# Softmax over 16384 rows of 512: the first load as even and odd partitions and the second as one DMA, both on SyncE's queue

## The chip, the cores and the metric

One core of one Trainium2 chip. The metric is the device time of one execution in microseconds (us). The kernel before takes 160.05 us (median; 159.97 to 160.12 in four runs). All runs were with a granted clock (the share of the full TensorE clock that the chip allowed) of 1.0. The profiled span, from the first to the last instruction, is about 1.4 us shorter than the time.

## The reference

```python
x: float32 [16, 1024, 512]
x_scaled = x / 2.0
exp_x = exp(x_scaled - max(x_scaled, axis=-1))
out = exp_x / sum(exp_x, axis=-1)            # float32
```

33.5 MB are read and 33.5 MB written, with a maximum, an exponential with its sum, and a multiplication in between.

## The kernel before

The 16384 rows are 128 rows in each of 128 partitions. They come in ten tiles of 3, 7, 13 and then 15 rows per partition, all in place in one arena of 98 rows in SBUF. VectorE takes the maximum, ScalarE the exponential with its sum, VectorE the reciprocal and the product, and SyncE (SP) issues the store. ScalarE (ACT) issues the loads, except load 0, which SyncE issues. Eight loads are issued at the start; the ninth and tenth reuse the arena's place and wait for stores. In the text "load 0" is the load of tile 0, and so on; a load has landed when its semaphore says that all of it is there. The first two are issued ahead of the program's entry barrier, the point at the start where the engines wait for one another. The code is cut:

```python
PLAN = [([3], 0), ([4, 3], 3), ([5, 4, 4], 10), ([5] * 3, 23), ...]   # chunks of rows, place in the arena
LAG = 2
SPREAD = 1

def issue_loads(begin, end):
    for t in range(begin, end):
        if t in behind:
            continue
        if t == 0:
            nc.sync.dma_start(out=sb(t), in_=dram(xf, t)).then_inc(ld[t], 16)
        elif t == SPREAD:
            r = tiles[t][1] - 1
            for p, q, lo, hi in ((0, P, 0, r), (0, 126, r, r + 1), (126, P, r, r + 1)):
                nc.scalar.dma_start(
                    out=sb(t)[p:q, lo:hi], in_=dram(xf, t)[p:q, lo:hi]
                ).then_inc(ld[t], 16)
        else:
            nc.scalar.dma_start(out=sb(t), in_=dram(xf, t)).then_inc(ld[t], 16)
...
for k in range(len(chunks) + LAG):          # VectorE
    if k < len(chunks):
        do_max(k)                           # waits for ld[t]
    if k >= LAG:
        do_mul(k - LAG)                     # waits for s_exp
for t in range(len(tiles)):                 # SyncE
    nc.sync.wait_ge(s_mul, last_chunk[t] + 1)
    nc.sync.dma_start(out=dram(of, t), in_=sb(t)).then_inc(...)
...
issue_loads(0, 2)                           # placed ahead of the entry barrier
...
issue_loads(2, len(tiles))                  # after it
```

So a row of load 0 (one partition's share) has 6144 bytes, of load 1 14336 (cut here into 12288 and 2048), of load 2 26624, of all others 30720.

## Time and profile before

| | before |
|---|---|
| time, us | 160.05 |
| bytes moved | 67.1 MB, 155.4 us at the 432 GB/s of the middle |
| VectorE, ScalarE busy | 83%, 60% of the span |
| load 0 issued, first row, landed | 0.00, 1.00, 6.2 us |
| load 1 issued, last row ended | 0.12, 8.28 us |
| last load's landing, last store issued | 127.6, 147.0 us |

The kernel is bound by its transfers; the prediction shows the lines. Two sources are used here. The views of the profile are quoted. The packet records of the trace (start, duration, size and queue of each row moved, without the engine's number) give times by row. Three sums over them, each divided by the 16 DMA engines, serve as a ledger:

- *idle*: time in which fewer than 16 rows were under way, from zero on;
- *slow*: what rows took beyond the usual for their size (84 ns for 2048 B, 158 for 4096, 234 for 6144, 460 for 12288, 535 for 14336, 987 for 26624, 1138 for 30720);
- the rest is rows at their usual pace, equal for all kernels but for 0.07 us.

Before: idle 1.18 us, all of it before 2 us, slow 0.57 up to 7 us, 0.45 from 7 to 10, 0.39 later.

### The profile page before, as it was taken

The page shows a single profiled execution, that of the slowest core. Times are in us where ns is not written, and L with a number is a line of the kernel's source. Part 1 is how long each engine was busy: PE and PEld are TensorE (multiplying, and loading weights), DVE is VectorE, ACT ScalarE, POOL GpSimd, SP SyncE. Part 2 cuts the span into 40 slices and gives each one's busy share as a digit, 9 for nine tenths or more (in the row PEclk, how much of TensorE's full clock was granted, in tenths as well). Part 3 has the DMA queues.
Part 4 walks back from the last instruction along what each step waited for, and adds up shares of the span by engine and source line. Part 5 has one row for each costly group of instructions (what it writes and reads, how often), then busy time and mean ns, then how long its engine had stood idle before and what let it go on. Part 6 is the DMA issues. An engine that isn't in the chain of part 4 may idle for free.

```text
span 158.6 us, 621 instructions
## 1 busy us (share of the span) xinstructions
DVE 131.4 (83%) x155; ACT 94.4 (60%) x257; POOL 0.2 (0%) x4
## 2 busy tenths in 40 slices
DVE  0466799999999999999999999996999389999000
ACT  0369197736874594669738797666566809763000
POOL 0000000000000000000000000000000000000000
DMA  7999999999999999999999999999999999999996
GB/s 268 449 373 430 414 431 466 435 407 399 466 443 389 434 463 448 418 444 426 442 426 434 426 426 442 426 441 411 457 395 472 395 473 395 472 395 465 395 472 263
DMA packets 3026, 67.13 MB, mean 423 GB/s; under 512 B 336, under 2 KB 336, under 8 KB 720
## 3 DMA queue, kind: packets, MB, share of 16 engines
q1 hardware_dynamic: 1584, 34.34, 50.6%
q10 hardware_dynamic: 1440, 32.77, 48.5%
q14 instruction: 2, 0.02, 0.0%
HBM read 33.55 MB, written 33.55 MB: 423 GB/s over the span
## 4 chain that ended last, share of the span: by engine, by line
DMA 52%; DVE 38%; issue 0%
DMA arena<-in_x_dram 38%; DVE stats L118 18%; DMA out_dram<-arena 14%; DVE arena L131 13%; DVE arena L138 7%; DVE recip L127 1%
## 5 line engine op out<-in xcount | busy, mean ns | idle before, releaser
L118 DVE TENSOR_REDUCE stats<-arena 128x5 f32<-128x2560 f32 (+2 forms) x27 | 72.2, 2676 | 14.6 <-DMA arena<-in_x_dram 14.6
L176 ACT ACTIVATE arena<-arena,stats 128x512 f32<-128x512 f32 x68 | 48.2, 710 | 23.4 <-DVE stats L118 23.4
L211 ACT ACTIVATE arena<-arena,stats x60 | 42.5, 710 | 20.7 <-ACTq L203 20.7
L138 DVE TENSOR_SCALAR arena<-arena,recip 128x512 f32<-128x512 f32 x93 | 38.6, 482 | 0.7
L131 DVE TENSOR_TENSOR arena<-arena,recip 128x2560 f32<-128x2560 f32 (+2 forms) x8 | 19.9, 2491 | 0.3
L176 ACT ACTIVATION_READ_ACCUMULATOR arena<-arena,stats 128x1 f32 x68 | 12.7, 187 | 0.0
L211 ACT ACTIVATION_READ_ACCUMULATOR arena<-arena,stats x60 | 11.2, 187 | 0.0
L127 DVE RECIPROCAL recip<-stats 128x5 f32<-128x5 f32 (+2 forms) x27 | 4.8, 177 | 0.0
L171 ACT ACT_TABLE_LOAD x1 | 1.3, 1283 | 5.7 <-issue 5.7
L252 POOL MEMSET const-bfloat16-1.0<- 128x1 bf16 x1 | 0.1, 101 | 0.0
L252 POOL MEMSET const-uint8-127<- 128x1 uint8 x1 | 0.1, 101 | 0.0
L252 POOL MEMSET const-float32-0.0<- 128x1 f32 x1 | 0.1, 98 | 0.2 <-issue 0.2
L252 POOL MEMSET const-float32-1.0<- 128x1 f32 x1 | 0.1, 98 | 0.0
## 6 DMA issues: line engine op xcount, KB each, us to landing
arena<-in_x_dram ACTq DMA_DIRECT2D x7, 3840.0 KB, 46.6
out_dram<-arena SPq DMA_DIRECT2D x7, 3840.0 KB, 22.7
arena<-in_x_dram ACTq DMA_DIRECT2D x1, 3328.0 KB, 14.3
out_dram<-arena SPq DMA_DIRECT2D x1, 3328.0 KB, 21.1
out_dram<-arena SPq DMA_DIRECT2D x1, 1792.0 KB, 18.2
arena<-in_x_dram ACTq DMA_DIRECT2D x1, 1536.0 KB
arena<-in_x_dram SPq DMA_DIRECT2D x1, 768.0 KB, 6.2
out_dram<-arena SPq DMA_DIRECT2D x1, 768.0 KB, 15.8
```

The costliest lines, as they stand in the source:

```text
L118: nc.vector.reduce_max(out=stats[:, b : b + c], in_=arena[:, a : a + c], axis=mybir.AxisListType.X, negate=True,)._wait_ge(ld[t], 48 if t ...
L127: nc.vector.reciprocal(out=recip[:, b : b + c], in_=stats[:, b : b + c])._wait_ge(s_exp, k + 1).then_inc(s_rec, 1)
L131: nc.vector.tensor_mul(out=arena[:, a : a + c], in0=arena[:, a : a + c], in1=recip[:, b : b + c].unsqueeze(2).to_broadcast([P, c, D]),)._w ...
L138: ins = nc.vector.tensor_scalar_mul(out=arena[:, a + r], in0=arena[:, a + r], scalar1=recip[:, b + r : b + r + 1],)
L171: nc.scalar.preload_act_table(mybir.ActivationFunctionType.Exp)
L176: ins = nc.scalar.activation(out=arena[:, a + r], in_=arena[:, a + r], func=mybir.ActivationFunctionType.Exp, bias=stats[:, b + r : b + r ...
L211: ins = nc.scalar.activation(out=data, in_=data, func=mybir.ActivationFunctionType.Exp, bias=stat, scale=0.5, accum_out=stat,)
L252: nc = _bacc.Bacc("TRN2", target_bir_lowering=False, num_devices=1)
```

## The change

Load 0 becomes two DMAs over the even and the odd partitions, load 1 a single one; all three go to SyncE's queue in order. The intent, as I read it, is to have the engines start evenly, so that the split over 126 and 2 partitions, which gave two late engines less work (they started load 0 at 1.62 and 1.75 us, the others at 1.00 to 1.25), isn't needed.

```diff
-SPREAD = 1
+HALVES = 2
             if t == 0:
+                for p in range(HALVES):
+                    nc.sync.dma_start(
+                        out=sb(t)[p:P:HALVES], in_=dram(xf, t)[p:P:HALVES]
+                    ).then_inc(ld[t], 16)
+            elif t == 1:
                 nc.sync.dma_start(out=sb(t), in_=dram(xf, t)).then_inc(ld[t], 16)
-            elif t == SPREAD:
-                r = tiles[t][1] - 1
-                for p, q, lo, hi in ((0, P, 0, r), (0, 126, r, r + 1), (126, P, r, r + 1)):
-                    nc.scalar.dma_start(
-                        out=sb(t)[p:q, lo:hi], in_=dram(xf, t)[p:q, lo:hi]
-                    ).then_inc(ld[t], 16)
...
-        )._wait_ge(ld[t], 48 if t == SPREAD else 16).then_inc(s_max, 1)
+        )._wait_ge(ld[t], 16 * HALVES if t == 0 else 16).then_inc(s_max, 1)
```

## The prediction

Passages that no trace or run of this case shows are cut from the text below, and the cuts are marked. -0.24 - 0.43 = -0.67 us gives 159.35, +0.18 - 0.43 = -0.25 us gives 159.77, and my forecast was 159.5. The -0.43 us itself stands on the trace (load 2's first rows took 1.34 to 1.49 us on all 16 engines, later ones 0.99, and nothing was lost at the step from 26624 to 30720 B). One correction from the same records: 14 engines have 84 ns rows just ahead of load 2, but two go straight from a 12288 B row to it, at 7.69 and 7.79 us (not 7.70), and lose the time too (1.49 and 1.45 us). The "two to four rows" of part 5 and the "20%" of the third rival are my estimates: the first from the 3.68 us between the issue of the first store (14.65) and its first row (18.33), the second assumed.

> **What bounds the kernel now.** I read the page first. It shows VectorE (DVE) busy for 83% of the span, ScalarE (ACT) for 60%, and the DMA row full in nearly every slice.
>
> ```profile
> span 158.6 us, 621 instructions
> DVE 131.4 (83%) x155; ACT 94.4 (60%) x257; POOL 0.2 (0%) x4
> DMA  7999999999999999999999999999999999999996
> DMA packets 3026, 67.13 MB, mean 423 GB/s; under 512 B 336, under 2 KB 336, under 8 KB 720
> ```
>
> The kernel moves 67.1 MB whatever its order, and only the first and last slice are not full. To see what the edges cost I asked for busy time by stretches; the columns are stretch, length, the busy time of three engines, clock, DMA share, GB/s.
>
> ```profile
> 0.00:2.00 2.00, 0.00 (x0) 0.00 (x0) 0.20 (x4) 1.00 0.48 126
> 2.00:4.00 2.00, 0.00 (x0) 0.00 (x0) 0.00 (x0) 1.00 1.03 418
> 6.00:8.00 2.00, 1.75 (x1) 1.03 (x1) 0.00 (x0) 1.00 1.38 496
> 8.00:10.00 2.00, 0.73 (x1) 1.99 (x5) 0.00 (x0) 1.00 0.69 270
> 18.00:126.00 108.00, 104.22 (x115) 74.80 (x206) 0.00 (x0) 1.00 1.01 432
> 140.00:156.00 16.00, 6.84 (x19) 3.64 (x10) 0.00 (x0) 1.00 1.00 432
> ```
>
> From 18 to 156 us the DMA engines run at 432 GB/s without a hole. At that rate all bytes take 67.1 MB / 432 GB/s = 155.4 us; the other 3.2 us of the span lie in the first 10 us and in the last. (6 to 8 and 8 to 10 average 383 GB/s, so that stretch too is below 432.)
>
> Next the chain of waits, in order of time, and the waits by length, which say whether the compute engines hold the end as well.
>
> ```profile
> 2.65 14.32 DMA arena<-in_x_dram
> 58.80 22.66 DMA out_dram<-arena
> 81.49 46.15 DMA arena<-in_x_dram
> 127.66 2.82 DVE stats L118
> 144.88 2.07 DVE arena L138 x5
> DVE stats L118 <- DMA arena<-in_x_dram: 14.6, 5, 6.2
> ```
>
> The chain takes the last load's landing (127.64 us), then 19.3 us of VectorE, then the last store (issued at 146.99, landed at about 158.3). The packet records of the trace (start, duration, size and queue of each row moved) qualify this: the last store's first row moves at 148.4, exactly when the store before it runs out. So the transfers hold the end, and VectorE's tail has only some 0.4 us to spare (1.4 us between issue and need, against the 1.0 us that the first load takes from issue to first byte). VectorE itself waited 1.42 us for the ninth tile (in the timeline at 109.49) and 3.29 us for the tenth (at 127.66): 4.7 us of reserve between 17 us and the tail.
>
> [...]
> - [...]126 rows go to 14 engines, 9 each, and 2 rows to 2. The trace agrees: ACT's eleven DMAs left 160 four-byte semaphore packets on its queue, which is 9 x 16 (nine of them have 128 partitions) + 14 + 2.
> - [...]between 2.5 and 5.4 us the 6144 B rows of load 0 (SP queue) and the 12288 B rows of load 1 (ACT queue) alternate on each engine.
> [...]
>
> **Why 126 and 2.** By joining row ends to row starts I sorted the packet records into 16 engines. Fourteen begin load 0 between 1.00 and 1.25 us, two at 1.62 and 1.75. These two reach load 2 first, at 7.69 and 7.70 us; the fourteen get there between 7.73 and 8.27. So the split gives the late starters 9 x 84 ns = 0.76 us less work, to make up for about 0.5 us of late start. The change takes this balance away and, I take it, tries to cure the late start itself: a first DMA of 64 rows gives each engine 4 rows instead of 8, so the last two may be served sooner.
>
> **The change, part by part.**
> 1. Rows. Per engine, loads 0 and 1 now take 8 x 234 + 8 x 460 + 9 x 84 = 6.31 us (ten short rows on the two that also take the 2-row DMA: 6.39). Afterwards they take 8 x 234 + 8 x 535 = 6.15 us (535 ns is what the 14336 B rows of the second store take). For the most loaded engines that is 0.24 us less.
> 2. The step from short rows to long ones. Load 2's first row takes 1.34 to 1.49 us on all 16 engines, later ones 0.99: 0.43 us lost on each, just after a run of 84 ns rows. Other steps (26624 to 30720 B) cost nothing (1.14 us first row and later). [...] After the change this should go: -0.43 us.
> 3. The late start. If the 64-row DMA cures it, all engines start by about 1.25 us and nothing is lost. If not, the two late engines now have as much work as the rest: 1.75 + 6.15 + 0.26 (their slower first row) + 0.3 (small gaps, as now) = 8.45 us, against 8.27 for the last engine now: +0.18 us.
> 4. Issues. SP gets two more before the entry barrier, ACT loses three. ACT's third issue ends at 1.48 us and delays the barrier; three SP issues of 0.38 end at 1.14. So load 2 is issued some 0.4 us earlier, at about 2.2 instead of 2.65. Worth nothing by itself, as the engines are busy with loads 0 and 1.
> 5. Order. Load 0 no longer shares with load 1: its last row ends at 1.1 + 0.4 + 8 x 0.234 = 3.4 us instead of 5.39, and VectorE starts at about 3.9 instead of 6.22. But load 1 moves from ACT's queue, where load 2 stood behind it, to SP's, where load 2 runs beside it. Load 2's first rows come after two to four rows of load 1 ([...]the first store was issued at 14.65 and moved at 18.33). Then the rest alternate, 0.535 + 0.99 us a pair. Load 1 ends at 3.4 + 8 x 0.535 + (4 to 6) x 0.99 = 11.6 to 13.6 us, where it now ends at 8.28. The second maximum starts at 12 to 14 instead of 9.27; the fourth, which now starts at 16.99 on load 2's landing, at 17.6 to 19.6.
>
> So VectorE gains 2.3 us, loses it again, and is 0.6 to 2.6 us later than now from the fourth maximum on. That fits in the reserve of 4.7 us. Stores start 3 to 5 us later, loads have the engines to themselves for longer, so the last load should land 0.5 to 1.5 us earlier than 127.64, which lengthens the tail's 0.4 us. None of part 5 is on the path, as the engines are never out of rows.
>
> **Sum.** Cured: -0.24 - 0.43 = -0.67 us, 159.35. Not cured: +0.18 - 0.43 = -0.25 us, 159.77. At 60 to 40: 159.5 us.
>
> **Rivals.**
> - *The late start stays, and the 0.43 us returns in another place* (at the first row of load 2 beside load 1, or between the two halves of load 0). Then the two unbalanced engines set the end: 160.02 + 0.18 = 160.2. For it: nothing in the trace shows what makes the two late. Against: when ACT's queue joined the busy engines at 2.5 us, most first rows took the usual 460 ns.
> - *Load 1's late landing becomes the bound.* For it: VectorE is 95% busy from 18 to 126 us, so a delay over the reserve goes straight to the last store, at 1 us for 1. Against: it takes 4.7 us, a start of the fourth maximum at about 21.7; at load 1's worst, ending with load 2 at 16, it would be at 20. If it did happen: 160.5 to 162.
> - *Writing every other partition is slower.* [...] Only 0.8 of 67 MB is touched; 20% slower rows would be 0.4 us: 159.9.
> - *All is hidden.* The last row's landing is what counts and the engines now finish within 0.7 us of each other (157.48 to 158.19); should one straggle for its own reasons, the gain is not seen: 160.0.
>
> **Range and chances.** The two sums give 159.35 and 159.77; rivals one, three and four end between 159.9 and 160.2, rival two above. The best that the start could give (1.0 us to first byte, 155.4 us of rows, about 0.5 us of first delay, 0.5 us of landing, and 1.4 us between span and time) is 158.8. So 158.9 to 160.2, eight times in ten. A 2% step is 3.2 us: faster is not in the bytes, and slower needs rival two at its worst.
>
> **What would show each step.** Packets: 3026 - 128 = 2898, those under 8 KB 592. First maximum at about 3.9 us; second at 12 to 14; the wait for the tenth tile's load down from 3.29 us; the first store issued at 18 to 20 instead of 14.65. The first rows of load 2 at 0.99 us, not 1.4. All 16 engines starting load 0 by 1.3 us, or two at 1.6 and later. The rate of 432 from 18 to 156 us unchanged. I am wrong if the transfers show a hole in the middle or before the last store (rival two), if the span moves by more than 1 us either way, or if load 1 lands before 9 us, which would mean that the queues don't alternate as I read it.

## The result, and the profile after

The changed kernel takes 161.34 us (161.21 to 161.71, four runs) against 160.05: ratio 1.0085, 95% interval 1.0067 to 1.0103. A ratio is the mean time of one kernel's fast runs over that of the other's of the same rounds, so not quite the ratio of the medians quoted. It is within 2%, but slower by 1.3 us, and above the predicted range.

The page of the changed kernel first. The count of packets came out as predicted; the first two slices of the DMA row, at 215 and 328 GB/s, are emptier.

```profile
span 159.9 us, 620 instructions
DMA  6899999999999999999999999999999999999995
DMA packets 2898, 67.13 MB, mean 420 GB/s; under 512 B 336, under 2 KB 336, under 8 KB 592
```

The timeline of the issues at the start (start, length from the first issue to the end of the last, queue, line, what, count), before and then after. Load 1 is what `L110` issues in both.

```profile
0.00 0.38 SPq L105 DMA_DIRECT2D arena<-in_x_dram  x1
0.12 1.36 ACTq L110 DMA_DIRECT2D arena<-in_x_dram  x3
2.65 3.07 ACTq L114 DMA_DIRECT2D arena<-in_x_dram  x6
```
```profile
0.00 1.18 SPq L106 DMA_DIRECT2D arena<-in_x_dram  x2
1.22 0.59 SPq L110 DMA_DIRECT2D arena<-in_x_dram  x1
2.87 3.86 ACTq L112 DMA_DIRECT2D arena<-in_x_dram  x6
```

Each half takes longer to issue (0.54 and 0.58 us) than the whole did (0.38). So load 1 is issued at 1.22 us instead of 0.12, SP reaches the barrier at 1.81, and load 2 is issued at 2.87.

Busy time by stretches of 1 us (the last two columns are the DMA engines' share and GB/s), before and then after:

```profile
3.00:4.00 1.00, 0.00 (x0) 0.00 (x0) 0.00 (x0) 1.00 1.01 406
4.00:5.00 1.00, 0.00 (x0) 0.00 (x0) 0.00 (x0) 1.00 1.06 436
5.00:6.00 1.00, 0.00 (x0) 0.26 (x1) 0.00 (x0) 1.00 1.03 418
```
```profile
3.00:4.00 1.00, 0.00 (x0) 0.00 (x0) 0.00 (x0) 1.00 0.91 301
4.00:5.00 1.00, 0.00 (x0) 0.00 (x0) 0.00 (x0) 1.00 0.69 199
5.00:6.00 1.00, 0.85 (x1) 0.00 (x0) 0.00 (x0) 1.00 0.86 330
6.00:7.00 1.00, 0.91 (x1) 0.24 (x1) 0.00 (x0) 1.00 0.93 328
18.00:126.00 108.00, 107.03 (x120) 77.41 (x214) 0.00 (x0) 1.00 1.00 431
```

This is a hole that the kernel before does not have. The middle, in the last line, is as full as before. By the packet records load 0's rows begin at 1.32 us, and on the last two engines at about 1.65 and 1.86 (the records name no engine, so the later starts are inferred), and those of its second half end on most engines between 3.6 and 3.9. Load 1's rows begin at 3.54 us on the earliest engine and above 5 us on the last few; load 2's first at 6.97.

The ledger, in us per engine:

| | before | after | difference |
|---|---|---|---|
| idle up to 2 us | 1.18 | 1.50 | +0.32 |
| idle from 2 to 7 us | 0.00 | 0.77 | +0.77 |
| slow rows up to 7 us | 0.57 | 1.02 | +0.45 |
| slow rows from 7 to 10 us | 0.45 | 0.04 | -0.41 |
| slow rows later | 0.39 | 0.22 | -0.17 |
| rows at their usual pace | | | -0.07 |
| sum | | | +0.89 |

The mean end of the 16 engines' last rows moves from 157.75 to 158.75 us (+1.0; what is missing in the sum are small gaps), and the last of them from 158.19 to 159.53, because the engines now end 1.4 us apart instead of 0.7. That is the 1.3 us, of which the ledger holds 0.9. What makes the ends more uneven isn't shown. Between 140 and 157 us the engines idle under 0.01 us in both kernels, so the last store, now issued at 147.46 instead of 146.98, doesn't leave them without rows.

VectorE, before and then after (timeline; in brackets the wait ahead of it):

```profile
6.22 1.75 DVE L118 TENSOR_REDUCE stats<-arena 128x3 f32<-128x1536 f32 x1 [6.22 <-DMA arena<-in_x_dram]
16.99 2.82 DVE L118 TENSOR_REDUCE stats<-arena 128x5 f32<-128x2560 f32 x1 [2.37 <-DMA arena<-in_x_dram]
127.66 2.82 DVE L118 TENSOR_REDUCE stats<-arena 128x5 f32<-128x2560 f32 x1 [3.29 <-DMA arena<-in_x_dram]
```
```profile
5.15 1.75 DVE L116 TENSOR_REDUCE stats<-arena 128x3 f32<-128x1536 f32 x1 [5.15 <-DMA arena<-in_x_dram]
14.67 3.95 DVE L116 TENSOR_REDUCE stats<-arena 128x4 f32<-128x2048 f32 x2 [7.76 <-DMA arena<-in_x_dram]
19.93 2.81 DVE L116 TENSOR_REDUCE stats<-arena 128x5 f32<-128x2560 f32 x1
128.15 2.82 DVE L116 TENSOR_REDUCE stats<-arena 128x5 f32<-128x2560 f32 x1 [2.34 <-DMA arena<-in_x_dram]
```

VectorE starts sooner (5.15 us), then waits until 14.67 us for load 1, and is 2.9 us later than before at its fourth maximum (19.93 against 16.99). It still waits 2.34 us for the tenth tile at the end.

### The profile page after: what moved, and what is told of

The parts are those of the page before. It is cut to its first block, busy times and chain, and to the rows that moved or that the text cites. A ratio compares the mean times of both kernels' runs of the same rounds, so it can differ in the third digit from the quotient of the medians.

```text
span 159.9 us, 620 instructions
## 1 busy us (share of the span) xinstructions
DVE 131.2 (82%) x155; ACT 94.4 (59%) x257; POOL 0.2 (0%) x4
## 4 chain that ended last, share of the span: by engine, by line
DMA 50%; DVE 41%; SPq 1%; issue 0%
DMA arena<-in_x_dram 36%; DVE stats L116 21%; DMA out_dram<-arena 14%; DVE arena L129 12%; DVE arena L136 7%; DVE recip L125 1%; SPq L106 1%
## 5 line engine op out<-in xcount | busy, mean ns | idle before, releaser
L209 ACT ACTIVATION_READ_ACCUMULATOR arena<-arena,stats x60 | 11.2, 187 | 0.0
```

What stands on the lines that cost most here:

```text
L209: ins = nc.scalar.activation(out=data, in_=data, func=mybir.ActivationFunctionType.Exp, bias=stat, scale=0.5, accum_out=stat,)
```

## The experiments

**Theories.** A: the engines lose time at the start because load 1's rows come too late, and they come late because load 1 is issued late. B: load 1, now running beside load 2, lands late and makes VectorE late, and that sets the end. C: the halves themselves are slow. All twelve kernels gave the right result. The twelve were timed against the kernel before, in four groups on four chips, each with its own runs of the kernel before (four to six runs of each kernel); in the table "issued" is the start of load 1's issue (of its long rows), and the last three columns are of the ledger, from one profiled run each. The columns don't add up to the time. How far the last engine ends behind the mean of the sixteen differs too, from 0.4 us (before, halves_act) over 0.8 to 0.9 (changed, one_sp, load1_held, load2_held, short_first) to 1.3 (two_columns, stores_late), and no run here tells why.

| run | time, us | ratio to before, 95% | issued | idle 2-7 | slow to 7 | slow after 10 |
|---|---|---|---|---|---|---|
| before | 160.05 | | 0.12 ACT | 0.00 | 0.57 | 0.39 |
| changed | 161.34 | 1.0085 (1.0067-1.0103) | 1.22 SP | 0.77 | 1.02 | 0.22 |
| one_sp | 160.38 | 1.0020 (1.0007-1.0033) | 0.43 SP | 0.01 | 0.46 | 1.14 |
| one_act | 160.18 | 1.0008 (0.9994-1.0021) | 0.12 ACT | 0.00 | 0.49 | 1.08 |
| halves_act | 160.28 | 1.0014 (1.0001-1.0027) | 0.12 ACT | 0.02 | 0.54 | 0.83 |
| halves_block | 161.51 | 1.0088 (1.0075-1.0101) | 1.22 SP | 0.13 | 1.85 | 0.20 |
| halves_two_queues | 160.73 | 1.0046 (1.0031-1.0060) | 0.60 SP | 0.23 | 0.33 | 0.97 |
| load1_held | 161.19 | 1.0070 (1.0056-1.0084) | 0.92 SP | 0.54 | 0.93 | 0.50 |
| load2_held | 160.48 | 1.0025 (1.0011-1.0039) | 0.43 SP | 0.01 | 0.53 | 1.01 |
| two_columns | 161.45 | 1.0075 (1.0061-1.0088) | 0.90 SP | 0.45 | 0.99 | 0.28 |
| short_first | 160.75 | 1.0038 (1.0024-1.0052) | 1.08 ACT | 0.15 | 0.97 | 0.47 |
| dve_late | 160.09 | 1.0003 (0.9989-1.0017) | 0.12 ACT | 0.00 | 0.55 | 0.47 |
| load2_early | 170.70 | 1.0670 (1.0655-1.0685) | 1.23 SP | 0.04 | 0.70 | 2.42 |
| stores_late | 161.41 | 1.0087 (1.0072-1.0102) | 0.12 ACT | 0.02 | 0.45 | 1.86 |

### First: the parts of the change, one at a time

**one_sp**: load 0 whole, load 1 still second on SP's queue.

```diff
-HALVES = 2
+HALVES = 1
```

> Changed kernel with load 0 as one DMA of 128 rows; load 1 stays whole, second on SP's queue. Theory A (rows reach the engines late because SP issues three DMAs in a row and each half takes as long to issue as a whole one, 0.54 to 0.59 us): load 1 is issued at about 0.45 instead of 1.22 us and load 2 at 2.3 to 2.5, the hole from 3.5 to 7 us (0.76 us of idle per engine) goes to under 0.2, time 159.9 to 160.4. Theory B (load 1 beside load 2 makes VectorE late and the tail long, wherever the rows start): load 1 still lands at 12 to 14 us, time stays at 161.0 to 161.5. Theory C (the strided halves themselves are slow): 159.6 to 160.2.

160.38 us: most of the loss is gone. Of one_sp's timeline and its stretches:

```profile
0.43 0.43 SPq L110 DMA_DIRECT2D arena<-in_x_dram  x1
```
```profile
3.00:4.00 1.00, 0.00 (x0) 0.00 (x0) 0.00 (x0) 1.00 1.25 518
4.00:5.00 1.00, 0.62 (x1) 0.14 (x1) 0.00 (x0) 1.00 1.02 416
```

Load 1 is there when load 0 ends (its first rows run at 3.2 us), and there is no hole. Load 1 still ends at 12.3 us and VectorE's second maximum starts at 13.63, as B needs, so B's 161.0 to 161.5 is refuted. The 0.3 us that is left is told apart from zero. In the profiled run it isn't idle time at the start: slow rows after 10 us rose by 0.75 us per engine (those from 7 to 10 fell by 0.44), and the last engine ends 0.9 us behind the mean instead of 0.4. Its cause stays open.

**one_act**: load 0 whole on SP, load 1 whole on ACT.

```diff
-HALVES = 2
+HALVES = 1
             elif t == 1:
-                nc.sync.dma_start(...)
+                nc.scalar.dma_start(...)
```

> Load 0 whole on SP, load 1 whole on ACT: the kernel before without its 126 and 2 split. My prediction's steps 1 to 3: the step from short to long rows (0.43 us) is gone, but the two late engines have as much work as the rest: 159.6 to 160.0. Theories A, B and C all expect no hole and load 1 landing at about 8 us. If it is above 160.2, the balance by the split was worth more than the lost 0.43 us.

160.18 us, not told apart from the kernel before, and outside what I expected (159.6 to 160.0). Load 2's first rows do take 0.99 us. But slow rows after 10 us rose from 0.39 to 1.08 us; more of this below.

**halves_act**: the halves on SP, load 1 whole on ACT.

```diff
             elif t == 1:
-                nc.sync.dma_start(...)
+                nc.scalar.dma_start(...)
```

> Load 0 as even and odd halves on SP, load 1 whole but on ACT's queue. Theory A: load 1 is issued at 0.12 us by ACT, its rows are there by 2.5 to 3 us, idle from 3.5 to 7 us under 0.2; start of the first rows at 1.3 us as in the changed kernel (0.3 us later than before); 159.9 to 160.4. Theory B: load 1 lands at 8 us, so 159.6 to 160.2. Theory C: the halves cost stays, 160.8 to 161.4.

160.28 us. The halves alone cost at the start what the changed kernel shows: first rows at 1.32 us, idle up to 2 us 1.51 against 1.18 in one_act. In the time that is 0.10 us, less than the intervals can tell. So C holds for a small part only.

**halves_block**: the halves as partitions 0 to 63 and 64 to 127.

```diff
-   out=sb(t)[p:P:HALVES], ...
+   out=sb(t)[p * P // HALVES : (p + 1) * P // HALVES], ...
```

> Changed kernel, but the two halves are partitions 0 to 63 and 64 to 127, not even and odd. Theories A and B: nothing changes, 161.0 to 161.6, issues of 0.54 to 0.59 us, hole from 3.5 to 7 us. Theory C (stride): issues fall to about 0.38 us, first row at 1.0 us, and the time to about 160.2.

161.51 us with the same issues (0.55, 0.58 and 0.59 us): the stride is not what makes them slow to issue. The start loses its time in another form, with less idle and more slow rows. Load 0's rows took 391 ns on average here and 283 with even and odd partitions (284 in the kernel before). Why rows of a block are slower isn't shown; no run here isolates it.

### Second: theory B by itself

**dve_late**: the kernel before, with VectorE held up ahead of its fourth maximum (the scratch tiles and their memset are left out below).

```diff
+            if k == 3:
+                for i in range(2):
+                    nc.vector.reduce_max(out=dump[:, 5*i:5*i+5], in_=zero (broadcast to 128x5x512), ...)
             if k < len(chunks):
                 do_max(k)
```

> The kernel before with two extra 2.73 us maxima over a scratch tile on VectorE just ahead of its fourth maximum, so that this starts at about 20 us instead of 16.99, as in the changed kernel (19.93); the loads are untouched. Theory A (only what the DMA engines lose at the start counts): the delay fits in VectorE's 4.7 us of reserve, 159.8 to 160.3, and the wait for the tenth tile's load shrinks to 1 to 3 us. Theory B (VectorE's lateness sets the end): 161.0 to 163.0. A wait for the tenth tile that is still above zero with an unchanged time speaks for A.

160.09 us, ratio 1.0003. The fourth maximum starts at 19.89 us, as late as in the changed kernel (19.93), and it costs nothing. Of its timeline:

```profile
14.44 5.54 DVE L157 TENSOR_REDUCE dump<-zero 128x5 f32<-128x2560 f32 x2
19.89 2.81 DVE L122 TENSOR_REDUCE stats<-arena 128x5 f32<-128x2560 f32 x1
```

And of its waits (total, times, longest):

```profile
DVE stats L122 <- DMA arena<-in_x_dram: 4.1, 2, 3.0
```

In all, VectorE now waits 4.1 us for loads instead of 14.6, none of it after 20 us (some of the first wait is now booked to the memset of the scratch tile, and the extra work fills the wait ahead of the fourth maximum). I had expected 1 to 3 us of waiting for the tenth tile to be left. There is none, because its load came sooner: its last row ends at 123.07 us, 3.1 us earlier than in the kernel before (126.17), and VectorE doesn't wait for it:

```profile
125.67 2.81 DVE L122 TENSOR_REDUCE stats<-arena 128x5 f32<-128x2560 f32 x1
```

So the delay of 2.9 us was taken by the reserve, and VectorE's tail even comes 2.0 us sooner (last store issued at 144.98 us instead of 146.98), which gains nothing either. B is refuted for delays of this size.

**load2_early**: the changed kernel with load 2 also ahead of the barrier, on ACT.

```diff
-    issue_loads(0, 2)
+    issue_loads(0, 3)
...
-    issue_loads(2, len(tiles))
+    issue_loads(3, len(tiles))
```

> Changed kernel, but ACT issues load 2 ahead of the entry barrier, at 0.12 instead of 2.87 us; SP's three issues stay as they are. If what counts is only that the engines have rows of any load (theory A), load 2 fills the hole from 3.5 to 7 us and the time falls to 160.0 to 160.6, although load 1 then lands even later (14 us or more), which theory B would expect to cost another 1 us or more (162). If load 2's rows stay behind the three SP DMAs (theory A2), the hole remains and the time is about 161.3.

170.70 us, a miss by 10 us, and the most instructive one. The hole is gone (idle from 2 to 7 us 0.04), as A expected. But load 2's rows reach the engines first (at 1.15 us, issued at 0.12 us by ACT, while load 0's first half, issued at 0.00 by SP, moves its first row at 3.70) and then alternate with load 0's, 987 ns against 234, so load 0 ends at 13.9 us and load 1 at 27.3. VectorE in its timeline:

```profile
15.43 1.75 DVE L116 TENSOR_REDUCE stats<-arena 128x3 f32<-128x1536 f32 x1 [15.43 <-DMA arena<-in_x_dram]
28.83 3.95 DVE L116 TENSOR_REDUCE stats<-arena 128x4 f32<-128x2048 f32 x2 [11.65 <-DMA arena<-in_x_dram]
34.09 2.81 DVE L116 TENSOR_REDUCE stats<-arena 128x5 f32<-128x2560 f32 x1
```

The fourth maximum is 17.1 us later than before. Take off the reserve of 4.7 and the 1.1 us by which the last store is now quicker (10.1 us from issue to its last row, instead of 11.2): 11.3 us, and the profiled span grew by 11.1. Beyond its reserve VectorE does set the end here, one for one, and the transfers then have holes near the end (DMA share 0.71 from 130 to 140 us and 0.46 from 140 to 150). Theory B's mechanism exists; the changed kernel doesn't reach it.

### Third: why load 1's rows come late

**halves_two_queues**: the odd half on ACT.

```diff
-                    nc.sync.dma_start(
+                    (nc.sync, nc.scalar)[p].dma_start(
```

> Changed kernel, but the odd half is issued by ACT; load 1 then is SP's second DMA, issued at 0.6 instead of 1.22 us. Theory A1 (rows come late because load 1 is the third in a row at one issuer): idle from 3.5 to 7 us falls from 0.76 to under 0.2, time 160.1 to 160.6. Theory A2 (three DMAs in flight at the start are too many for whatever makes the rows, whichever engine issues them): idle stays over 0.5 and the time over 161.

160.73 us. Load 1 is issued at 0.60 us and its rows begin at 3.62 to 4.3 us; load 0's rows on SP's queue end by 3.54 us and those on ACT's by 4.47, so the engines idle 0.23 us from 2 to 7 us instead of 0.77. This is just outside what I gave for A1 (under 0.2 us, 160.1 to 160.6) and far from A2 (over 0.5 us, over 161). Three DMAs are in flight at the start as in the changed kernel, so their number alone (A2) doesn't make the hole.

**load1_held**: one_sp with load 1's issue held until a GpSimd memset is done (the scratch tile and the semaphore are left out below).

```diff
             elif t == 1:
+                nc.gpsimd.memset(scratch[:, :], 0.0).then_inc(s_hold, 1)
+                nc.sync.wait_ge(s_hold, 1)
                 nc.sync.dma_start(...)
```

> one_sp (load 0 whole on SP, load 1 SP's second DMA; 160.38), but SP waits for a GpSimd memset before it issues load 1, which moves the issue from 0.43 to about 1.0 to 1.3 us, as in the changed kernel (1.22). Load 0's rows run out at 3.2 us. If what counts is when load 1 is issued (rows come 2.3 to 3 us later), the engines run dry from 3.2 until 3.5 to 4.2 us: 0.3 to 0.8 us of idle per engine between 2 and 7 us, time 160.7 to 161.2. If what counts is that it is the third DMA on one queue, or that the ones ahead are halves, there is no idle and the time is 160.3 to 160.5.

161.19 us: issuing load 1 0.48 us later costs 0.8 us and brings back the hole. Of its timeline and its stretches:

```profile
0.92 0.33 SPq L114 DMA_DIRECT2D arena<-in_x_dram  x1
```
```profile
3.00:4.00 1.00, 0.00 (x0) 0.00 (x0) 0.00 (x0) 1.00 0.92 315
4.00:5.00 1.00, 0.61 (x1) 0.00 (x0) 0.00 (x0) 1.00 0.88 258
```

**load2_held**: in load1_held the barrier, and so load 2, moved too (1.92 to 2.31 us). Here load 2 alone is held.

```diff
             elif t == 1:
+                for i in range(3):
+                    nc.gpsimd.memset(scratch[:, i], 0.0)     # SP does not wait for it
                 nc.sync.dma_start(...)
```

> one_sp again (160.38), with nothing held but load 2: three GpSimd memsets ahead of the entry barrier put its issue from 1.92 to about 2.9 us, as in the changed kernel (2.87); load 1 is still issued at 0.43 us. In load1_held load 2 was 0.39 us later too, so this tells the two apart. If load 1's issue is what opens the hole: under 0.1 us of idle between 2 and 7 us and 160.2 to 160.6. If load 2's lateness opens it: 0.3 us or more of idle and 160.8 to 161.3.

Of its timeline and its stretches:

```profile
0.43 0.42 SPq L113 DMA_DIRECT2D arena<-in_x_dram  x1
2.76 2.88 ACTq L115 DMA_DIRECT2D arena<-in_x_dram  x6
```
```profile
3.50:7.00 3.50, 1.75 (x1) 1.32 (x2) 0.00 (x0) 1.00 1.08 449
```

Load 2 is issued at 2.76 us, there is no hole (0.01 us), and the time is 160.48 us. So load 1's issue is the cause of the hole, not load 2's.

**two_columns**: load 0 cut by columns, so that both parts have 128 partitions.

```diff
-   out=sb(t)[p:P:HALVES], in_=dram(xf, t)[p:P:HALVES]
+   out=sb(t)[:, 2 * p : 2 + p], in_=dram(xf, t)[:, 2 * p : 2 + p]
```

> Changed kernel, but load 0 is cut by columns (two rows of each partition, then the third), so that both DMAs have 128 partitions; load 1 is still SP's third DMA. If a 64-partition DMA is what is slow, these two issue in 0.38 us each and start at 1.0 us, load 1 is issued at 0.85 us, and the hole from 3.5 to 7 us is under 0.3: 160.2 to 160.8. If third in a row is what is slow, the hole stays at 0.5 or more and the time is 161 or more.

161.45 us, above the 160.2 to 160.8 that I gave to "a 64-partition DMA is slow". The issues are indeed quick (0.38 and 0.43 us) and the first row is at 1.02, but load 1 is issued at 0.90, and that is late enough: the same as load1_held, where it is second in the queue and issued at 0.92 (161.19). In these two runs the time of its issue counts more than what stands ahead of it.

**short_first**: the kernel before, with the order of load 1's three DMAs turned, to keep its balance and lose the step from short to long rows.

```diff
-   ((0, P, 0, r), (0, 126, r, r + 1), (126, P, r, r + 1))
+   ((0, 126, r, r + 1), (126, P, r, r + 1), (0, P, 0, r))
```

In the expectation "my reading" is that the 0.43 us goes with the 84 ns rows ahead of load 2; the guess at why is cut.

> The kernel before with ACT's three DMAs for load 1 in another order: the 126 and 2 short rows first, the 12288 B rows last. The balance of the two late engines stays, and long rows stand ahead of load 2, so if my reading of the 0.43 us step holds[...], load 2's first row takes 0.99 us instead of 1.4 and idle at the start is unchanged. Time 159.5 to 159.8 if nothing takes the gain back; 159.9 to 160.3 if slow rows between 18 and 45 us do, as in one_act.

160.75 us, another miss, by the same cause: now the long rows of load 1 are issued at 1.08 us, behind the two short DMAs (0.64 and 0.24 us), and come at 3.9 to 4.7. Four engines' first long rows take over 1.3 us. This is ACT's queue, so late first rows aren't a matter of SP's alone. Load 2's first row takes 0.99 us after these long rows: the 0.43 us in the kernel before goes with load 1's short rows coming last, although two of its engines had no short row ahead and lost it too (1.49 and 1.45 us).

Put together, in these runs a DMA that followed another at the start, on either queue, got its first row moving 2.1 to 3.1 us after the start of its issue (two_columns' second DMA, 0.43 to 2.50; one_act, 0.12 to 2.46; changed kernel, 1.22 to 3.54; halves_block, 1.22 to 4.30), and its last engine after up to about 5 (changed kernel), although the first DMA to move needed 1.00 in the kernel before and 1.32 in the changed one. Which DMA that is doesn't follow from the order of issue alone: in load2_early it was the second one issued. Load 0 keeps the engines supplied until 3.2 us or so (one_sp). Issues at 0.43 us and before left no hole (idle from 2 to 7 us 0.00 to 0.02), those at 0.90 and later a hole or a run of slow first rows (idle 0.13 to 0.77 and slow rows 0.93 to 1.85; load2_early, where load 2 filled in, aside), the one at 0.60 a small hole (0.23). Why the later one needs so much longer isn't shown.

### Fourth: where one_act's gain went

**stores_late**: one_act with the first two stores held until the third is ready.

```diff
-            nc.sync.wait_ge(s_mul, last_chunk[t] + 1)
+            nc.sync.wait_ge(s_mul, last_chunk[max(t, 2)] + 1)
```

> Load 0 whole on SP, load 1 whole on ACT (as in one_act, 160.18), and the first two stores held back until the third is ready at 41 us. In one_act the rows of loads 3 to 5 took up to 0.3 us more at a few moments between 19 and 45 us, together 0.78 us per engine, all while the first two stores with their short rows (6144 and 14336 B) ran; that is where the 0.43 us won at the start seems to have gone. If the short store rows beside long load rows cause it, the extra moves to after 41 us or stays (160.0 to 160.3); if it is a matter of the time at which the two streams meet, it goes, and the time is 159.3 to 159.8.

161.41 us, outside both expectations. Slow rows before 41 us vanish, but 1.86 us of them appear later, nearly all between 41 and 95 us. One side effect muddles it: ACT waited 12.5 us for the held stores before it could issue load 8. What the two runs show is that slow rows after 10 us came at times at which stores ran beside loads: none before 41 us with the stores held, 0.78 us between 19 and 45 us in one_act. Which meetings of the two are slow stays open: one_act's own six runs spread from 159.90 to 160.63 us, and apart from stores_late and load2_early the kernels with 0.8 us or more of slow rows after 10 us are those whose load 1 was supplied in time, or nearly, as one DMA (one_sp, one_act, halves_act, load2_held, halves_two_queues). No run here beats the kernel before.

## Why the prediction was wrong

- *What bounds the kernel* was right: the transfers. The engines lost 0.9 us by the ledger and ended less evenly, and the time moved by 1.3 us, over the 1 us that the prediction named as a sign of being wrong.
- *Rows* (part 1) and *the step from short to long rows* (part 2) were right in size: -0.24 us for the most loaded engines is -0.07 on average over the engines, and of -0.43 us predicted 0.41 was measured (slow rows from 7 to 10 us, 0.45 to 0.04). short_first confirms that the step goes with load 1's short rows coming last (0.99 us for load 2's first row with the order turned); why is not shown, and two engines without a short row ahead lost it too. A long load 1 issued at 0.12 us (one_act) gives this up again in slow rows after 10 us (0.39 to 1.08): the gain is hidden, as in the fourth rival, but by another cause, which stays open.
- *The late start* (part 3) was wrong both ways. The 64-row DMA neither cures it nor leaves things as they were: the engines start between 1.32 and about 1.86 us, instead of 1.00 to 1.25 and two up to 1.75. This costs 0.32 us of idle, a cost I hadn't listed.
- *Issues* (part 4) was wrong: I took 0.38 us for each of SP's three from the one that I had seen, of a 128-partition DMA. They took 0.54, 0.58 and 0.59, so load 2 was issued 0.2 us later, not 0.4 earlier.
- *Order* (part 5) holds the step that failed: "None of part 5 is on the path, as the engines are never out of rows." I let load 1's rows follow load 0's at 3.4 us, as if a DMA issued at about 0.8 us were ready 1 us later like the first. It was issued at 1.22 and its rows came 2.3 us after that at the earliest, and the engines idled 0.77 us and had 0.45 us of slow rows. load1_held, load2_held and one_sp show that the time of load 1's issue makes this hole. A sign was in the profile before: ACT's load 1, issued at 0.12 us, moved its first row at 2.46, and I took delays of this kind (the first store, 14.65 to 18.33) for time spent on the rows of other DMAs, which was my estimate and is not shown. For VectorE's first maximum the same part gave 3.9 us; it came at 5.15, as the halves moved later and load 0's last row ended at 4.83 us instead of 3.4.
- *Load 1's late landing* was predicted in kind, and a little too early (second maximum at 12 to 14 us, measured 14.67; fourth at 17.6 to 19.6, measured 19.93; first store at 18 to 20, issued at 20.04). That it is harmless was right, as dve_late shows. The rival built on it is refuted here, and load2_early agrees with its limit of 4.7 us. The third rival, slower strided rows, is refuted by load 0's rows of 283 ns against 284 before.
- *The last load's landing* was to come 0.5 to 1.5 us earlier; it came 0.5 later (128.12). The idea is borne out by dve_late, where VectorE is as late, there is no hole, and the load's last row ends 3.1 us earlier than before. In the changed kernel it ends at 126.62 us, 3.55 after that of dve_late. The hole is part of this; the rest isn't shown. So it is luck that the wait for the tenth tile fell to 2.34 us as predicted: VectorE came later, not the load sooner.
- *The range* ended at 160.2, because in each rival only a known cost stayed or returned. None of them had the engines without rows at the start.
- *Two slips in the working* changed nothing: VectorE's 104.22 us of 108 are 96.5% and not 95%, and the sum in part 3 is 8.46 and not 8.45.

## What to carry to other kernels

Where transfers bound a kernel, count at its start not only what each engine must move but when it can move it: issue the second DMA within some tenths of a microsecond of the first, from the other queue if need be, and don't put a third issue ahead of it. Here 0.43 us was soon enough, 0.60 not quite and 0.90 too late, with a first load whose rows lasted until about 3.2 us; a first load of another size was not tried. Starting the compute earlier was worth nothing here, as VectorE had reserve (one_sp starts it at 4.38 us instead of 6.22 and is no faster). Here two queues shared an engine mostly row by row, so a load with long rows issued too early starved the one that was needed first (load2_early: 987 ns rows between those of 234 ns, load 0 ended at 13.9 us instead of 5.39). To keep loads in order of need on one queue avoided this in the kernel before: load 2's first rows began at 7.69 to 8.27 us, and load 1's last ended at 8.28.

## What the runs show of issues, first rows and steps

- First rows: in the kernel before, the first DMA's first row moved 0.62 us after the end of its issue (0.38 to 1.00 us). Later DMAs at the start needed 2.1 to 3.1 us from the start of their issue to their first row (two_columns 0.43 to 2.50, one_act 0.12 to 2.46, changed kernel 1.22 to 3.54, halves_two_queues 0.60 to 3.62 us), and longer on other engines (load1_held 0.92 to 3.24 on four engines, 3.74 and later on the others). In load2_early the DMA issued first needed 3.70 us.
- Two queues: rows of 6144 and 12288 B (kernel before, 2.5 to 5.4 us), and of 26624 and 14336 (changed kernel, 7 to 13 us), alternate mostly one by one, at times two by one, as far as rows can be joined into engines.
- Issue times ahead of the barrier: 0.33 (load1_held) to 0.43 us (one_sp) for DMAs of 128 partitions, but 0.57 (halves_two_queues) to 0.59 (changed kernel) behind halves on SP, and 0.73 in load2_early; 0.54 to 0.58 for 64 partitions, strided (changed kernel) or not (halves_block), 0.64 to 0.67 for 126 and 0.24 for 2 (short_first, kernel before).
- The step from short rows to long ones: 0.35 to 0.45 us on 14 engines from 84 ns rows to 26624 B rows (kernel before), but also 0.46 and 0.50 on the two that came from 12288 B rows there; none on most engines from 12288 or 14336 B rows (short_first and one_act 0.99 us; changed kernel 0.99 to 1.00 on 13 of 16 engines, 1.13 to 1.20 on three, as joined).
- Halves: in halves_act they put off the first row by 0.3 us (1.32 instead of 1.00) and gained nothing (160.28 us against 160.18 of one_act). The even and odd halves' rows, at 283 ns, were no slower than the whole load's 284, while those of partitions 0 to 63 and 64 to 127 took 391.
